# A SwiGLU FFN in 2x2 block algebra: two weight sums moved into accumulating DMAs, and 18 of 22 gate/up tiles in the algebra in place of 14

## The chip, the core and the metric

The kernel runs on one core of one Trainium2 chip. The metric is the device time of one execution in microseconds, taken as the median over several runs. Profiles are of one execution each, so a profile has a time of its own.

## The reference

One layer of a hybrid decoder, in float32: a token mixer (a gated recurrence and a gated delta rule side by side), then a feed-forward network. The change touches only the feed-forward network:

```
v = rms_norm(h, pre_ffn_w)                          # (512 tokens, 1024)
gate, up = split(v @ w_gate_up, 2)                  # w_gate_up: (1024, 2 * 2816)
f = (silu(gate) * up) @ w_down                      # w_down: (2816, 1024)
out = h + rms_norm(f, post_ffn_w)
```

Matrix products are made in about float32 accuracy: each operand x is split into a high part (x rounded to fp32r, the tiles `whi`, `vhi`) and a low part (x minus the high part, `wlo`, `vlo`), and a product is three fp32r matmuls, high x high, high x low and low x high.

## The kernel before

The program is written for one core with a scheduler that sets the order on each engine and inserts the waits; a tile pool hands out buffers in turn, and a new tile waits until the last reader of the tile that had the buffer before it is done. Pools that matter here: `raw` (fresh weights, float32) has 2 buffers, `whi` and `wlo` (the split weights) have 3 each. ScalarE (ACT) makes every high part, VectorE (DVE) every low part. SyncE's queue (SP) issues the loads, in its order: a load whose buffer is not free holds back the loads behind it. GpSimd (POOL) has a queue of its own for DMAs.

The stages are: mixers, merge, output projection (`out_proj`), FFN gate/up (`ffn`), FFN down (`down`). In `ffn` the 2816 columns of gate and of up are 22 tiles `ft` of 128. A tile's weights are `w_gu[ft, 0]` (gate) and `w_gu[ft, 1]` (up), each 128 x 1024 (512 KB): the first 512 columns are the four blocks of 128 inputs of the upper half of the 1024 inputs, the other 512 those of the lower half. There are two kinds of tile.

- A **direct** tile loads gate and up with `wload` (one DMA of 512 KB each into a `raw` buffer, a split of 128x1024 on ACT and on DVE), and TensorE makes 2 x 8 x 3 = 48 matmuls of 512 columns (L116 to L118).
- A **Winograd** tile takes gate and up times the two halves of the inputs and the two halves of the tokens as a 2x2 block product with 7 products in place of 8 (`winograd`, L959). Each product is 4 x 3 = 12 matmuls of 256 columns (L1010 to L1012). Its seven weight operands, numbered 0 to 6, are blocks or sums of blocks; each is split by `operand` (L913) into half a `whi` and half a `wlo` buffer (128x512), so three buffers hold six operands, and a pair of operands waits for the products of the third pair before it. TensorE takes a tile's products in the order 0, 1, then 6 of the tile before, then 2, 3, 4, 5; `s15`, `s16`, `c22`, `c12`, `c21` are its evictions on DVE (128x256), and `flush` ends the tile before (silu and product).

Before, the four weight sums are made by DVE in `winograd`: two at once into `t13` (128x1024), then two into `t24` (128x512 each). Both are tiles of the pool `raw`:

```
self.tt(t13, raw[:, 1:3], raw[:, 0:2], ALU.subtract)
self.tt(t24[:, 0], B22, t13[:, 0], ALU.subtract)
self.tt(t24[:, 1], B21, t24[:, 0], ALU.subtract)
```

The name `raw` in `winograd` is something else: a slot of 128x4x512, one of two that take turns, `s` in the profile; four loads of 256 KB fill it. Tiles 0, 1, 4, 7, 10, 13, 16 and 19 are direct (`ft < 2 or ft % 3 == 1`), so the other 14 come in twos, a direct tile between.

Of the kernel before, what the change touches and what calls it, by code (L numbers as in the profile page):

```python
# [9 lines left out]
F32 = mybir.dt.float32  # L10
# [4 lines left out]
ALU = mybir.AluOpType  # L15

P = 128
# [6 lines left out]
NF = DFF // P  # L24
EPS = 1e-6
NEG = -30000.0
HG_LEVELS = (64, 32, 16, 8, 4, 2, 1)
HG_MASKS = (16, 8, 4, 2, 1)

# [14 lines left out]
class K:  # L44
# [570 lines left out]
    def hg_attn(self, c, out):  # L615
# [20 lines left out]
        yield  # L636
        for lev in HG_LEVELS[:-1]:
            v = lambda x: x.rearrange("p h (n two t) -> p (h n) two t", two=2, t=lev)
# [194 lines left out]
    def out_proj(self):  # L833
# [4 lines left out]
        for nh in range(2):  # L838
            for lst, tile_, nm in ((pmw, self.hct, "post_mix_w"), (pfw, self.st, "pre_ffn_w")):
                t = tile_()  # L840
                lst.append(t.rearrange("p h t -> p (h t)"))
                nc.gpsimd.dma_start(out=lst[nh], in_=self.I[nm][nh * 512:nh * 512 + 512].partition_broadcast(P))
        W = []
        for i in range(8):
# [9 lines left out]
            for j in range(2):  # L854
                raw = self.dct((P, 512))
                nc.sync.dma_start(out=raw, in_=self.I["w_out"][i, :, j * 512:j * 512 + 512])
                self.split(h_[:, j, :], l_[:, j, :], raw, nc.gpsimd if i % 2 else None)
            W.append((h_, l_))
        self.h = []
# [64 lines left out]
    def block_sums(self, A, tmp, dst):  # L924


        hi, lo = A
        H, L = slice(256, 512), slice(0, 256)
        g = self.nc.gpsimd
        out = dict(A11=(0, L), A12=(1, L), A22=(1, H))  # L930
        out = {n: [[x[i][:, k, t] for k in range(4)] for x in A] for n, (i, t) in out.items()}
        S_ = [([], []) for _ in range(4)]
        for j in (slice(0, 2), slice(2, 4)):
            def block(i, t, eng=None):
                a = tmp()
                self.tt(a, hi[i][:, j, t].bitcast(F32), lo[i][:, j, t].bitcast(F32), ALU.add, eng)
                return a

            def put(i, src):
                d = dst(i, j)  # L940
                self.split(d[0], d[1], src)
                for o, x in zip(S_[i], d):
                    o += [x[:, 0], x[:, 1]]

            a21, a22 = block(0, H), block(1, H)
            self.tt(a22, a21, a22, ALU.add)
            put(0, a22)
            a11 = block(0, L, g)
            self.tt(a21, a11, a21, ALU.subtract)
            put(2, a21)  # L950
            self.tt(a22, a22, a11, ALU.subtract)
            put(1, a22)
            a12 = block(1, L, g)
            self.tt(a12, a12, a22, ALU.subtract)
            put(3, a12)
        out.update({f"S{i + 1}": S_[i] for i in range(4)})
        return out

    def winograd(self, raw, A, c12, c21, c22):  # L959

        nc = self.nc
        with self.tc.high_priority(offset=200):
            B11, _, B22, B21 = (raw[:, i] for i in range(4))
            t13, t24 = (self.wp.tile([P, 1040], F32, tag="raw", name=self.name("raw"), bufs=2)[:, :1024]
                        .rearrange("p (i n) -> p i n", i=2) for _ in range(2))
            self.tt(t13, raw[:, 1:3], raw[:, 0:2], ALU.subtract)
            self.tt(t24[:, 0], B22, t13[:, 0], ALU.subtract)
            self.tt(t24[:, 1], B21, t24[:, 0], ALU.subtract)  # L970
            W = [[t.rearrange("p (k f) -> p k f", k=4) for t in self.operand(x)]
                 for x in (B11, t13[:, 0], t24[:, 0], B21, t13[:, 1], B22, t24[:, 1])]
        X, Wb, Y = (f((P, 256)) for f in (self.mm_ps, self.dps, self.hps))
        prod = lambda i, a, ps, start: self.product(i, W[i], A[a], ps, start)
        s1, s15, s16 = (self.ftmp() for _ in range(3))
        now = self.tc.high_priority

        def first():
            prod(0, "A11", X, True)
            with now():  # L980
                nc.scalar.copy(s1, X)
            prod(1, "S1", Wb, True)
            with now():
                self.tt(s15, Wb, s1, ALU.add)

        def second():
            prod(2, "S2", Y, True)
            with now():
                self.tt(s16, Y, s1, ALU.add)
            prod(3, "A12", X, False)  # L990
            prod(4, "S3", Y, False)
            with now():
                self.tt(c22, Y, s15, ALU.add)
            prod(5, "S4", Wb, False)
            with now():
                self.tt(c12, Wb, s16, ALU.add)

        def third():
            prod(6, "A22", Y, False)
            with now():  # L1000
                self.tt(c21, Y, s1, ALU.add)

        return X, first, second, third

    def product(self, i, W, A, ps, start):
        wh, wl = W
        ah, al = A
# [14 lines left out]
    def ffn(self):  # L1022

        nc = self.nc
        A = nc.scalar
        self.half = self.fhalf = None
        gt = []

        def gslot(i):
            if i % 4 == 0:  # L1030
                gt.append(self.slot((4, 13, 11, 12, 14, 15)[i // 4], [P, 4, S]))
            return gt[i // 4][:, i % 4, :]

        def mms(ps, w, ts):
            for k in range(KD):
                self.mm3(ps[:, ts], w[0][:, k, :], w[1][:, k, :], self.vhi[k // 4][:, k % 4, ts],
                         self.vlo[k // 4][:, k % 4, ts], k == 0, k == KD - 1)

        load = lambda ft, gu: self.wload(self.I["w_gu"][ft, gu], (P, KD, P))

        def evac(t, g, u):
            with self.tc.high_priority():
                self.sigmoid(t, g)
                self.tt(t, t, g, ALU.mult)
                self.tt(t, t, u, ALU.mult)

        bank = lambda gu: self.hps((P, 512)) if gu else self.mm_ps()

        first = [(0, 0), (0, 1), (1, 0)]
        ws = {p: load(*p) for p in first}  # L1050
        pss = {p: bank(p[1]) for p in first}
        for half in range(2):
            for p in first:
                mms(pss[p], ws[p], slice(half * 256, half * 256 + 256))
        sp = [self.slot(i, [P, 4, 2, 256]) for i in (14, 15)]
        sp = iter([t[:, i] for t in sp for i in range(4)])
        so = [self.slot(i, [P, 2, 4, 256], F32R) for i in range(4)]
        L = self.block_sums((self.vhi, self.vlo), lambda: next(sp), lambda i, j: (so[i][:, 0, j], so[i][:, 1, j]))
        lo, hi = slice(0, 256), slice(256, 512)
        pending = None  # L1060

        def flush():
            nonlocal pending
            if pending:
                X, third, g, u, t = pending
                third()
                A.activation(t[:, lo], X, AF.Exp, scale=-1.0)
                A.activation(t[:, hi], g[:, hi], AF.Exp, scale=-1.0)
                A.activation(t, t, AF.Ln, bias=self.one)
                A.activation(t, t, AF.Exp, scale=-1.0)  # L1070
                self.tt(t[:, lo], t[:, lo], X, ALU.mult)
                self.tt(t[:, hi], t[:, hi], g[:, hi], ALU.mult)
                self.tt(t, t, u, ALU.mult)
            pending = None

        for ft in range(NF):
            if ft < 2 or ft % 3 == 1:
                for gu in range(2):
                    if (ft, gu) not in ws:
                        pss[ft, gu] = bank(gu)  # L1080
                        mms(pss[ft, gu], load(ft, gu), slice(0, S))
                    if gu == 0:
                        flush()
                evac(gslot(ft), pss[ft, 0], pss[ft, 1])
                continue
            with self.tc.high_priority():
                raw = self.slot(5 + ft % 2, [P, 4, 512])

                for gu in range(2):
                    src = self.I["w_gu"][ft, gu].rearrange("p (a b) -> p a b", a=2)  # L1090
                    nc.sync.dma_start(out=raw[:, gu], in_=src[:, 0])
                    nc.sync.dma_start(out=raw[:, 3 - gu], in_=src[:, 1])
            g, u = self.hct((P, 512)), self.hct((P, 512))
            X, p1, p2, p3 = self.winograd(raw, L, u[:, lo], g[:, hi], u[:, hi])
            p1()
            flush()
            p2()
            pending = X, p3, g, u, gslot(ft)
        flush()
        self.gt = gt  # L1100
# [116 lines left out]
def layouts(i):  # L1217
# [28 lines left out]
    t = np.arange(P)  # L1246
    cm = [np.eye(P), t[:, None] <= t[None, :], np.where(t[:, None] <= t[None, :], 0.0, NEG)]
    blk = lambda h: ((t[:, None] // (2 * h) == t[None, :] // (2 * h))
# [22 lines left out]
```

## Time and profile before

| | |
|---|---|
| median of 3 runs | 860.11 us (859.06 to 862.14) |
| the profiled execution | 856.85 us, its span 855.1 us |
| FFN gate/up, first direct matmul to first matmul of the down stage | 482.36 to 715.53 us of the span |
| of it the steady stretch, tiles 4 to 20 | 526.37 to 712.00 us, six periods of one direct and two Winograd tiles |
| FFN down | 715.53 to about 847 us |

The span runs from the first to the last instruction; 1.75 us lie outside it. A period of the steady stretch begins with the first 512-column matmul of a direct tile.

### The profile page before, as it was taken

Reading aid. Unit: us, or ns where it says so; the run is one execution under the profiler, and the core shown is the slowest. Engines: PE = TensorE matmul, PEld = TensorE weight load, DVE = VectorE, ACT = ScalarE, POOL = GpSimd, SP = SyncE. Lnnn points to the kernel's source line nnn. Section 1 sums busy time; section 2 is a strip of 40 time slices with the busy share of each in tenths; the row PEclk is TensorE's granted clock in tenths of the full one; section 3 lists DMA queues with packets and bytes.
Section 4 is the critical chain, followed back from the end, with each engine's and each line's share of the span. In section 5 each row is a group of like instructions: output and inputs, shape, how many; then the busy total and the mean of one; then the engine's idle time right before and its main releaser. Section 6 shows DMA issues by size and latency. Waiting matters only on the chain.

```text
span 855.1 us, 12329 instructions
## 1 busy us (share of the span) xinstructions
PE 823.5 (96%) x4684; PEld 695.8 (81%) x4684; DVE 581.2 (68%) x903; ACT 487.2 (57%) x888; POOL 137.4 (16%) x182
## 2 busy tenths in 40 slices
PE   8998999999999998999999999999999999999995
PEld 8986887788877777888888898999999998876774
DVE  4598779518478788622574697787787787557545
ACT  6648788755475666755443464545555456445443
POOL 1320168300054545300010300000000000000000
PEclk9999999959999999999999999999999999999999
DMA  8425432501051123522211313232322405556552
GB/s 295 152 75 196 125 101 95 155 26 50 26 185 50 50 75 99 170 91 88 96 62 50 124 41 109 91 107 99 122 76 100 148 5 168 174 173 212 182 170 101
DMA packets 34315, 96.43 MB, mean 113 GB/s; under 512 B 4112, under 2 KB 4528, under 8 KB 34128
## 3 DMA queue, kind: packets, MB, share of 16 engines
q1 hardware_dynamic: 32112, 88.65, 31.5%
q0 software_dynamic: 2144, 6.99, 3.1%
q8 instruction: 37, 0.61, 0.3%
q14 instruction: 22, 0.18, 0.1%
HBM read 90.90 MB, written 4.73 MB: 112 GB/s over the span
## 4 chain that ended last, share of the span: by engine, by line
PE 56%; DMA 11%; DVE 9%; POOL 4%; ACT 4%; issue 3%; DVEq 0%; ACTq 0%; SPq 0%; POOLq 0%
DMA raw<-in_w_down_dram 8%; PE mm L117 7%; PE mm L118 7%; PE mm L116 7%; POOL s L147 4%; DVE wlo L109 4%; ACT whi L108 3%; DVE hct L147 2%; PE hps L1011 2%; PE hps L1010 2%; PE hps L1012 2%; PE mm L869 2%; PE mm L868 2%; PE mm L867 2%; PE hps L118 2%
## 5 line engine op out<-in xcount | busy, mean ns | idle before, releaser
L109 DVE TENSOR_TENSOR wlo<-raw,whi 128x1024 fp32r<-128x1024 f32 x108 | 135.7, 1257 | 121.3 <-ACT whi L108 120.2
L116 PE MATMUL mm<-s,whi 128*128 128x512 f32 (+1 forms) x496 | 195.3, 394 | 0.0
L117 PE MATMUL mm<-s,whi 128*128 128x512 f32 (+1 forms) x496 | 195.0, 393 | 0.0
L118 PE MATMUL mm<-s,wlo 128*128 128x512 f32 (+1 forms) x496 | 194.6, 392 | 0.1
L108 ACT CAST whi<-raw 128x1024 fp32r<-128x1024 f32 x108 | 113.0, 1046 | 92.3 <-PE mm L117 39.1
L118 PEld LDWEIGHTS mm<-s,wlo 128*128 128x128 f32 x496 | 94.0, 190 | 19.8 <-DVE wlo L109 0.6
L116 PEld LDWEIGHTS mm<-s,whi 128*128 128x128 f32 x496 | 94.2, 190 | 19.3 <-issue 0.2
L117 PEld LDWEIGHTS mm<-s,whi 128*128 128x128 f32 x496 | 94.1, 190 | 18.7
L147 POOL TENSOR_TENSOR s<-s,dct 128x512 f32<-128x512 f32 (+1 forms) x9 | 12.7, 1435 | 391.6 <-DVE s L150 360.6
L121 ACT CAST whi<-raw 128x512 fp32r<-128x512 f32 (+1 forms) x64 | 38.9, 617 | 30.2 <-PE mm L1011 10.1
L121 ACT CAST whi<-s 128x512 fp32r<-128x512 f32 x42 | 25.9, 617 | 47.1 <-PE mm L117 21.4
L1010 PE MATMUL hps<-s,whi 128*128 128x256 f32 x168 | 47.2, 281 | 0.4 <-DVE hct L147 0.4
L1011 PE MATMUL hps<-s,whi 128*128 128x256 f32 x168 | 47.2, 281 | 0.1
L1012 PE MATMUL hps<-s,wlo 128*128 128x256 f32 x168 | 46.9, 279 | 0.0
L147 POOL TENSOR_TENSOR hct<-s 128x256 f32<-128x256 f32 (+1 forms) x55 | 43.4, 818 | 21.3 <-DVE hct L147 8.3
L147 DVE TENSOR_TENSOR wlo<-raw,whi 128x512 fp32r<-128x512 f32 (+1 forms) x64 | 43.5, 688 | 3.9 <-ACT whi L121 3.0
L147 DVE TENSOR_TENSOR hct<-hct,s 128x256 f32<-128x256 f32 (+1 forms) x63 | 32.7, 559 | 2.0 <-ACT hct L609 1.0
L147 POOL TENSOR_TENSOR s<-s 128x126 f32<-128x126 f32 (+22 forms) x62 | 32.3, 521 | 9.7 <-DMA s<-scr 4.9
L1010 PEld LDWEIGHTS hps<-s,whi 128*128 128x128 f32 x168 | 31.5, 188 | 0.9 <-DVE hct L147 0.6
L1011 PEld LDWEIGHTS hps<-s,whi 128*128 128x128 f32 x168 | 31.6, 188 | 0.6 <-DVE s L147 0.3
L1012 PEld LDWEIGHTS hps<-s,wlo 128*128 128x128 f32 x168 | 31.7, 189 | 0.0
L1011 PE MATMUL mm<-s,whi 128*128 128x256 f32 x112 | 31.5, 281 | 0.0
(329 smaller groups left out, 1943.2 us busy)
## 6 DMA issues: line engine op xcount, KB each, us to landing
raw<-in_w_in_a_dram SPq DMA_DIRECT2D x44, 512.0 KB, 3.4
raw<-in_w_down_dram SPq DMA_DIRECT2D x44, 512.0 KB, 3.4
s<-in_w_gu_dram SPq DMA_DIRECT2D x56, 256.0 KB, 4.0
raw<-in_w_gu_dram SPq DMA_DIRECT2D x16, 512.0 KB, 3.5
raw<-in_w_o_dram SPq DMA_DIRECT2D x8, 512.0 KB, 3.4
dct<-in_w_out_dram SPq DMA_DIRECT2D x16, 256.0 KB, 3.4
raw<-in_w_iab_dram SPq DMA_DIRECT2D x8, 260.0 KB, 5.9
s<-in_xT_dram SPq DMA_DIRECT2D x8, 256.0 KB, 6.0
```

What stands on the lines that cost most here:

```text
L108: nc.scalar.copy(hi[:, :n], raw[:, :n])
L109: nc.vector.tensor_tensor(out=lo[:, :n], in0=raw[:, :n], in1=hi[:, :n].bitcast(F32), op=ALU.subtract)
L116: mm(ps, lh, rh, start=start, stop=False)
L117: mm(ps, lh, rl, start=False, stop=False)
L118: return mm(ps, ll, rh, start=False, stop=stop)
L121: self.nc.scalar.copy(hi, src)
L147: (eng or self.nc.vector).tensor_tensor(out=out, in0=a, in1=b, op=op)
L867: T.matmul(ps, mh, wh, start=k == 0, stop=False)
L868: T.matmul(ps, mh, wl, start=False, stop=False)
L1010: mm(ps, wh[:, k, :], ah[k], start=start and k == 0, stop=False, skip_group_check=True)
L1011: mm(ps, wh[:, k, :], al[k], start=False, stop=False, skip_group_check=True)
L1012: mm(ps, wl[:, k, :], ah[k], start=False, stop=k == 3, skip_group_check=True)
```

## The change

1. **Two sums by DMA.** Per Winograd tile, a tile `u13` of the pool `raw` (128x2x512) is loaded by SP with the first halves of gate and up (512 KB). Then GpSimd issues a DMA that adds the whole of up (512 KB from DRAM) to it: `u13[0]` becomes gate's first half plus up's first, `u13[1]` up's first plus up's second. The slot's loads are one of 512 KB (gate) and one of 256 KB (up's second half).
2. **The other two sums** stay on DVE, in place in the slot (128x512 each): `U2 = B22 + u13[0]`, and `B21 = B21 + U2` once operand 3, which is the old B21, is split.
3. **Signs** in `block_sums` and in three evictions follow, so that the sums are plus.
4. **Direct tiles** are 0, 1, 8 and 15. The 18 Winograd tiles come in runs of six: 2 to 7, 9 to 14, 16 to 21.

```diff
+DIRECT = (0, 1, 8, 15)
...
-    def winograd(self, raw, A, c12, c21, c22):
+    def winograd(self, raw, u13, A, c12, c21, c22):
...
-            B11, _, B22, B21 = (raw[:, i] for i in range(4))
-            t13, t24 = (self.wp.tile([P, 1040], F32, tag="raw", name=self.name("raw"), bufs=2)[:, :1024]
-                        .rearrange("p (i n) -> p i n", i=2) for _ in range(2))
-            self.tt(t13, raw[:, 1:3], raw[:, 0:2], ALU.subtract)
-            self.tt(t24[:, 0], B22, t13[:, 0], ALU.subtract)
-            self.tt(t24[:, 1], B21, t24[:, 0], ALU.subtract)
-            W = [[t.rearrange("p (k f) -> p k f", k=4) for t in self.operand(x)]
-                 for x in (B11, t13[:, 0], t24[:, 0], B21, t13[:, 1], B22, t24[:, 1])]
+            B11, B21, B22, U2 = (raw[:, i] for i in range(4))
+            self.tt(U2, B22, u13[:, 0], ALU.add)
+            W = [self.operand(x) for x in (B11, u13[:, 0], U2, B21, u13[:, 1], B22)]
+            self.tt(B21, B21, U2, ALU.add)
+            W = [[t.rearrange("p (k f) -> p k f", k=4) for t in w] for w in W + [self.operand(B21)]]
...
-            if ft < 2 or ft % 3 == 1:
+            if ft in DIRECT:
...
                 raw = self.slot(5 + ft % 2, [P, 4, 512])
-
-                for gu in range(2):
-                    src = self.I["w_gu"][ft, gu].rearrange("p (a b) -> p a b", a=2)
-                    nc.sync.dma_start(out=raw[:, gu], in_=src[:, 0])
-                    nc.sync.dma_start(out=raw[:, 3 - gu], in_=src[:, 1])
+                u13 = self.wp.tile([P, 1040], F32, tag="raw", name=self.name("raw"), bufs=2)[:, :1024]
+                u13 = u13.rearrange("p (i n) -> p i n", i=2)
+                g, u = (self.I["w_gu"][ft, gu].rearrange("p (a b) -> p a b", a=2) for gu in range(2))
+                nc.sync.dma_start(out=u13, in_=self.I["w_gu"][ft, :, :, :512].rearrange("g p n -> p g n"))
+                nc.sync.dma_start(out=raw[:, :2], in_=g)
+                nc.sync.dma_start(out=raw[:, 2], in_=u[:, 1])
+
+                nc.gpsimd.dma_start(out=u13, in_=u, accum_op=ALU.add)
```

Every line number behind the first hunk is one higher than before. The next lists show an engine's instructions in program order: line, operation, tile written, tiles read, shape. Here `raw_n` is a tile of the pool `raw` and `s_n` the slot of a Winograd tile.

DVE before the change, tiles 8 (`raw_5112`, `raw_5113`) and 9 (`raw_5229`, `raw_5230`, `s_792_5222`): the three sums of tile 9 stand among the low parts (`wlo`) of tile 8 and its evictions (`hct` from `dps` or `hps`).

```order
L147 TENSOR_TENSOR wlo_5130<-raw_5112,whi_5129 128x512
L147 TENSOR_TENSOR wlo_5130<-s_773_5105,whi_5129 128x512
L147 TENSOR_TENSOR raw_5229<-s_792_5222 128x1024
L147 TENSOR_TENSOR hct_5142<-dps_5140,hct_5142 128x256
L147 TENSOR_TENSOR wlo_5136<-raw_5113,whi_5135 128x512
L147 TENSOR_TENSOR wlo_5136<-s_792_5222,whi_5135 128x512
L147 TENSOR_TENSOR hct_5143<-hps_5141,hct_5142 128x256
L147 TENSOR_TENSOR raw_5230<-s_792_5222,raw_5229 128x512
L147 TENSOR_TENSOR raw_5230<-s_792_5222,raw_5230 128x512
```

DVE after the change, in the run 9 to 14, tiles 11 (`raw_5542`) and 12 (`raw_5676`, `s_841_5675`): U2 of tile 12 is the third row, s15 of tile 11 the fifth, operand 4 of tile 11 (`u13[1]`) the sixth.

```order
L148 TENSOR_TENSOR hct_5417<-dps_5441,hct_5443 128x256
L148 TENSOR_TENSOR s_824_5541<-s_824_5541 128x512
L148 TENSOR_TENSOR s_841_5675<-s_841_5675,raw_5676 128x512
L148 TENSOR_TENSOR s_792_5290<-s_792_5290,hct_5303 128x512
L148 TENSOR_TENSOR hct_5576<-dps_5574,hct_5576 128x256
L148 TENSOR_TENSOR wlo_5563<-raw_5542,whi_5562 128x512
L148 TENSOR_TENSOR wlo_5563<-s_824_5541,whi_5562 128x512
```

The three sums of a tile (one of 1024, two of 512) have become two of 512, the first of which (U2) reads the accumulated `u13`; it stands ahead of operand 4 of the tile before it, which is the last reader of that tile's `u13`.

DVE after the change at the start of the first run, tiles 3 (`raw_4547`, `s_707_4546`) and 4 (`raw_4678`, `s_721_4677`):

```order
L148 TENSOR_TENSOR hct_4439<-hct_4467,hps_4466 128x256
L148 TENSOR_TENSOR hct_4439<-dps_4465,hct_4468 128x256
L148 TENSOR_TENSOR s_721_4677<-s_721_4677,raw_4678 128x512
L148 TENSOR_TENSOR wlo_4564<-s_707_4546,whi_4563 128x512
L148 TENSOR_TENSOR wlo_4564<-raw_4547,whi_4563 128x512
L148 TENSOR_TENSOR s_707_4546<-s_707_4546 128x512
```

U2 of tile 4 stands ahead of operands 3 and 4 of tile 3 (the low parts `wlo_4564`). Before the change tile 4 was direct and had no sum there.

SP's queue after the change, tiles 11 and 12; L1089 is the load of `u13`, L1090 and L1091 fill the slot:

```order
L1089 DMA raw_5542<-in_w_gu_dram 128x2x512
L1090 DMA s_824_5541<-in_w_gu_dram 128x1024
L1091 DMA s_824_5541<-in_w_gu_dram 128x512
L1089 DMA raw_5676<-in_w_gu_dram 128x2x512
L1090 DMA s_841_5675<-in_w_gu_dram 128x1024
L1091 DMA s_841_5675<-in_w_gu_dram 128x512
```

A tile has three loads here where it had four of 256 KB, and the load of `u13` has come in ahead of the slot's; the accumulating DMA (L1093) is alone on GpSimd's queue, whose other work between the first Winograd tile's and the last's is four adds of `block_sums` and one load of `post_ffn_w`, all ahead of the second accumulation.

## Rows read from the trace of the kernel before

**Rows 1.** The page: the span, and each engine's busy time.

```profile
span 855.1 us, 12329 instructions
PE 823.5 (96%) x4684; PEld 695.8 (81%) x4684; DVE 581.2 (68%) x903; ACT 487.2 (57%) x888; POOL 137.4 (16%) x182
```

**Rows 2.** Busy time per stretch: one period, the whole steady stretch, the down stage.

```profile
core 0: us, PE busy (x) PEld busy (x) DVE busy (x) ACT busy (x) POOL busy (x), PEclk, DMA share, GB/s
557.59:588.50 30.91, 30.91 (x218) 28.83 (x217) 24.26 (x41) 15.99 (x29) 0.00 (x0) 1.00 0.29 100
...
526.37:712.00 185.63, 185.51 (x1299) 172.73 (x1297) 145.93 (x242) 96.20 (x175) 0.00 (x0) 1.00 0.29 97
716.00:842.00 126.00, 121.56 (x513) 94.03 (x512) 72.49 (x100) 62.12 (x98) 0.00 (x0) 1.00 0.55 178
```

**Rows 3.** TensorE in order of time: start, length, line, tile; first matmuls of blocks.

```profile
588.50 0.40 PE L116 MATMUL mm<-s,whi 128*128 128x512 f32 x1
...
594.05 0.28 PE L1010 MATMUL hps<-s,whi 128*128 128x256 f32 x1
...
595.49 0.39 PE L116 MATMUL hps<-s,whi 128*128 128x512 f32 x1
...
601.03 0.28 PE L1010 MATMUL mm<-s,whi 128*128 128x256 f32 x1
...
609.47 0.28 PE L1010 MATMUL mm<-s,whi 128*128 128x256 f32 x1
```

**Rows 4.** DVE in order of time, back to back, in Winograd tiles.

```profile
602.43 0.68 DVE L147 TENSOR_TENSOR wlo<-s,whi 128x512 fp32r<-128x512 f32 x1
603.03 1.22 DVE L147 TENSOR_TENSOR raw<-s 128x1024 f32<-128x1024 f32 x1
604.17 0.42 DVE L147 TENSOR_TENSOR hct<-dps,hct 128x256 f32<-128x256 f32 x1
...
618.09 0.42 DVE L147 TENSOR_TENSOR s<-s,hct 128x256 f32<-128x256 f32 x1
618.43 0.42 DVE L147 TENSOR_TENSOR hct<-hps,hct 128x256 f32<-128x256 f32 x1
```

**Rows 5.** DMA issues: queue, count, KB each, median us from issue to landing.

```profile
s<-in_w_gu_dram SPq DMA_DIRECT2D x40, 256.0 KB, 4.0
raw<-in_w_gu_dram SPq DMA_DIRECT2D x10, 512.0 KB, 3.6
...
s<-gd POOLq DMA_DIRECT2D x1, 1024.0 KB, 6.5
scr<-dct POOLq DMA_DIRECT2D x1, 1024.0 KB, 9.3
scr<-s POOLq DMA_DIRECT2D x2, 512.0 KB, 3.8
st<-in_pre_ffn_w_dram POOLq DMA_DIRECT2D x2, 256.0 KB, 3.6
```

**Rows 6.** Start of the Winograd tiles: DVE and TensorE in order of time.

```profile
497.99 1.21 DVE L109 TENSOR_TENSOR wlo<-raw,whi 128x1024 fp32r<-128x1024 f32 x1
506.88 0.28 PE L1010 MATMUL mm<-s,whi 128*128 128x256 f32 x1
```

**Rows 7.** Start of the down stage: last Winograd matmul, ScalarE, first down matmul.

```profile
713.30 0.28 PE L1012 MATMUL hps<-s,wlo 128*128 128x256 f32 x1
...
714.13 1.04 ACT L108 CAST whi<-raw 128x1024 fp32r<-128x1024 f32 x1 [1.30 <-DVE wlo L109]
715.08 1.01 ACT L121 CAST hct<-s 128x256 fp32r<-128x256 f32 x3
...
715.53 0.50 PE L1121 MATMUL dps<-whi,hct 128*128 128x512 f32 x1 [1.95 <-ACT hct L121]
```

**Rows 8.** All that GpSimd does from 470 to 720 us.

```profile
478.73 6.02 POOL L147 TENSOR_TENSOR s<-s,s 128x512 f32<-128x512 f32 x4 [46.29 <-PE mm L868]
488.36 0.55 POOL L1131 DMA_DIRECT2D st<-in_post_ffn_w_dram  x1 [3.62 <-DVE hct L150]
```

More of the change, by code (lines that the diff above doesn't have):

```diff
@@ L945, in block_sums @@
             a21, a22 = block(0, H), block(1, H)
-            self.tt(a22, a21, a22, ALU.add)
+            self.tt(a22, a21, a22, ALU.subtract)
             put(0, a22)
@@ L953, in block_sums @@
             a12 = block(1, L, g)
-            self.tt(a12, a12, a22, ALU.subtract)
+            self.tt(a12, a12, a22, ALU.add)
             put(3, a12)
@@ L983, in first @@
             with now():
-                self.tt(s15, Wb, s1, ALU.add)
+                self.tt(s15, Wb, s1, ALU.subtract)
         def second():
@@ L992, in second @@
             with now():
-                self.tt(c22, Y, s15, ALU.add)
+                self.tt(c22, s15, Y, ALU.subtract)
             prod(5, "S4", Wb, False)
             with now():
-                self.tt(c12, Wb, s16, ALU.add)
+                self.tt(c12, Wb, s16, ALU.subtract)
         def third():
@@ L1087, in ffn @@
                 raw = self.slot(5 + ft % 2, [P, 4, 512])
-                for gu in range(2):
-                    src = self.I["w_gu"][ft, gu].rearrange("p (a b) -> p a b", a=2)
-                    nc.sync.dma_start(out=raw[:, gu], in_=src[:, 0])
-                    nc.sync.dma_start(out=raw[:, 3 - gu], in_=src[:, 1])
+                u13 = self.wp.tile([P, 1040], F32, tag="raw", name=self.name("raw"), bufs=2)[:, :1024]
[5 more added lines that the diff above has]
+                nc.gpsimd.dma_start(out=u13, in_=u, accum_op=ALU.add)
             g, u = self.hct((P, 512)), self.hct((P, 512))
-            X, p1, p2, p3 = self.winograd(raw, L, u[:, lo], g[:, hi], u[:, hi])
+            X, p1, p2, p3 = self.winograd(raw, u13, L, u[:, lo], g[:, hi], u[:, hi])
             p1()
```

## The prediction

> **What bounds the kernel now.** I read the page first: TensorE is busy 96% of the span [rows 1]. Ends of matmuls are modelled there, so this alone proves little. Second, busy time by stage: in the steady stretch of the FFN TensorE is busy 185.51 of 185.63 us at clock 1.00, DVE 145.93 (79%), ACT 96.20 (52%), the DMA engines 29%, GpSimd nothing [rows 2]. Third, to be sure that TensorE sets the pace, I read its starts: gate of a direct tile starts at 588.50 and the next block at 594.05, up at 595.49 and the next at 601.03 [rows 3]. That is 5.55 and 5.54 us for 24 matmuls each, 0.231 us apart. From 601.03 to 609.47 lie six products, 1.41 us each, and the seventh takes 594.05 to 595.49. The period made of these (11.09 + 2 x 9.88 = 30.85) is the period measured, 30.91 [rows 2]. So nothing waits there, and what counts is how many matmuls TensorE is given, as long as its operands come in time.
>
> **The change part by part.** Spans of one profiled execution make the sum; that execution took 856.85 us, 3.26 below the median of 860.11, and the result is carried over to the median.
>
> *Products.* A direct tile costs 11.09 us, a Winograd tile 8.44 + 1.44 = 9.88 [rows 3]. Four tiles change kind: 4 x 1.21 = **4.8 us less**, if TensorE stays fed.
>
> *DVE.* Back to back, a 128x512 operation follows the one before by 0.60 us, one of 128x1024 by 1.14, one of 128x256 by 0.34 [rows 4]. A Winograd tile before is 1.14 + 2 x 0.60 for sums, 7 x 0.60 for low parts, 5 x 0.34 for evictions, and 2 x 0.34 + 0.60 to end the tile before: 9.5 us. After, the 1.14 is gone: 8.4 us per 9.88 of TensorE, 85%. In runs of six there is no direct tile to catch up in, but work alone leaves 1.5 us a tile. Before, 9.5 of 9.88 would have left little; so the runs rest on the DMA sums. I cost this at nothing, hidden behind the products. ACT has the same seven casts a tile and 48% to spare. The changed signs cost nothing: the same operations.
>
> *DMA traffic.* A tile moved 1 MB and now moves 1.75 MB, 0.5 of it added to what is there. At 29% load [rows 2] this fits by volume; the down stage runs at 55% and lands its loads. The SP queue gives up a load a tile; GpSimd's has no work behind the accumulations until the end but one load [rows 8], so its wait for `u13` holds up nobody.
>
> *The new wait.* Call L the time from a free `u13` buffer to U2's input: the load (512 KB, 3.6 us by the `raw` row [rows 5]; the nearest with rows of 2 KB is the slot's, 4.0 in bursts of four), two hand-overs of about 0.1 us (my estimate), and X, the accumulation. The trace has none. Below, X is a plain GpSimd DMA of 512 KB, 3.8 us; above, the slowest of 1024 KB, 9.3 [rows 5]. An accumulation reads the tile as well as DRAM. From 256 KB (3.6) to 1024 KB (6.5) 768 KB more cost 2.9 us, so 512 KB more read cost 1.9: I take X = 3.8 + 1.9 = **5.7**, L = 3.6 + 0.2 + 5.7 = **9.5**, with 7.6 and 13.1 for the ends.
>
> The Trainium skill, "Collectives: The Full Stack", section "The bandwidth ceiling: the fold count and why AG ≠ RS ≠ AR", says that an add in the DMA path costs no time for the adding, but needs two source reads that share one ring, and so runs at half a copy's rate. With its 31 GB/s an engine, X would by my estimate be 3.8 + 1.1 = 4.9 and the sum below 0.6 us better, at most; no row here shows an accumulation.
>
> U2 is what waits, and DVE works in order: everything behind U2 waits too. At the start of a run and at every other tile inside it, U2 of the next tile stands ahead of operand 4 of this one, which frees the buffer that the tile after next needs. So waits form a chain: U2, operand 4, L, U2. First run: the direct weight's low part frees tile 3's buffer at 499.2 [rows 6]. Then U2(3) at 499.2 + L, operand 4 of tile 2 2.5 later (three operations and its own 0.69), U2(4) after another L, operand 4 of tile 3 1.9 later, U2(5) after L, operand 4 of tile 4 2.2 later, U2(6) after L: 505.8 + 4L. Behind U2(6) stand two evictions and operand 5 of tile 5, 2.0 us, for the 27th product of the run: 506.88 [rows 6] + 26 x 1.41 + 1.9 of delay (next paragraph) = 545.4. So L may be 9.4. In the later runs tiles 9 and 10 have a direct tile's time for their sums; the chain starts with operand 4 of tile 9, 1.4 us after the direct tile's last matmul, and has three links: 1.4 + 2 x 2.2 + 3L against 26 x 1.41 - 2.0 = 34.7, L at most 9.6. Beyond **about 9.5** each microsecond of L costs 4 + 3 + 3 = 10 us; below it nothing. My L lies on the edge.
>
> *Start of the first run.* Before, the 13 products from 506.88 to 526.37, where the steady stretch begins [rows 2, 6], took 19.49 us, 1.2 more than 13 x 1.41. After, U2(3) holds DVE until 499.2 + 9.5 = 508.7; U2, four more operations and then the half of a block sum that product 2 needs half-way through take 5 x 0.60 + 0.69 = 3.7, to 512.4, where 510.4 would be in time (506.88 + 2.5 x 1.41): 1.9 late. That is **0.7 more**.
>
> *Start of the down stage.* The last product's last matmul starts at 713.30, the first of the down stage at 715.53: ACT makes the third down weight's high part at 714.13, held by DVE's low part of the second, and only then the left operand [rows 7]. The third's buffer is free when the last product ends (713.30 + 0.28, so 713.6). `u13` is done with two operands before `t24` was, so the first down weights load earlier, DVE is through with the second sooner, and I take **0.5 less**; nothing, if ACT's order finds another wait.
>
> Sum: -4.8 + 0.7 - 0.5 = **-4.6 us**: 852.25 in the profile, 855.5 as a median.
>
> **The rivals.** 0.3% (2.6 us) is about what a measurement of this kernel can tell from no change.
>
> *The accumulation is late (slower).* If X is 7.0, as a little above the 6.5 row, L is 10.8, the chains cost 13, and the sum is +8.4: 868.5. It decides from X = 6.2, where 10 x 0.46 eats the 4.6; at 9.3 (L 13.1) it would be 36 - 4.6, 891. For it: both 1024 KB rows exceed 6.2, 6.5 and 9.3 [rows 5], slot loads run in the same microseconds, and one late U2 delays the next buffer. Against it: the 3.8 row, and 71% idle DMA engines.
>
> *The chains eat the gain (same).* X between 5.9 and 6.4: 858 to 863.
>
> *DVE becomes the bound (same).* At 8.4 of 9.88 us every wait on an eviction in the middle of a tile costs slack. If a Winograd tile took 10.2 us, 18 x 0.32 = 5.8 would cancel the products: 861.3. Against it: before, two tiles of 9.5 followed each other with no gap on TensorE.
>
> *The accumulation is quick (faster still).* X = 3.8: U2(3) at 506.8, the start is in time, and its 1.2 us of delay are gained: -4.8 - 1.2 - 0.5 = -6.5, 853.6.
>
> **How the numbers follow.** Forecast 0.38, quick accumulation 0.10, the two that end in no change 0.20 together, late accumulation 0.32. Faster is 0.48, same 0.20, slower 0.32. The likeliest case's own range is 853.5 to 857.5. For 8 in 10 the low end is 853 (a quick accumulation; 0.05 below it) and the high end 870, the chains at L = 10.95; 0.12 lies beyond, towards 891.
>
> **What would show it.** Right: in the steady part of a run seven products every 9.88 us with no idle time of TensorE; U2 (`s<-s,raw`) in DVE's list with idle time released by the accumulating DMA, some microseconds per tile at a run's start, and operands still in time; accumulations landing in 5 to 6 us. Wrong: TensorE idle before a Winograd matmul, released by a low part, at the fourth or fifth tile of each run; that would be the late accumulation, its landing above 6.2. DVE busy without gaps while TensorE waits would be the DVE rival. If U2 never waits, the quick one holds. The sum would be wrong in its first term if a product in a run took other than 1.41 us.

## The result

The changed kernel takes **885.58 us** (median of 4 runs, 884.14 to 892.9), beside 859.59 us of the kernel before on the same chip: 1.0318 times as long, 95% interval 1.0254 to 1.0381. The prediction, 855.5 with a range up to 870, was wrong; of its rivals the late accumulation comes nearest in mechanism and time.

The profiled execution took 884.97 us, its span is 883.2. From its page: span and busy time [rows 1]; three groups of instructions (busy, mean ns | idle time ahead of them, and what ended it); DMA issues [rows 5].

```profile
span 883.2 us, 12751 instructions
...
PE 831.1 (94%) x4828; PEld 707.4 (80%) x4828; DVE 578.4 (65%) x941; ACT 497.6 (56%) x916; POOL 153.0 (17%) x200
...
L1008 PE MATMUL hps<-s,whi 128*128 128x256 f32 x216 | 63.7, 295 | 21.0 <-DVE hct L148 20.7
...
L1093 POOL DMA_DIRECT2D raw<-in_w_gu_dram x18 | 15.6, 864 | 224.8 <-DVE wlo L148 116.5
L148 DVE TENSOR_TENSOR s<-s,raw 128x512 f32<-128x512 f32 x18 | 12.5, 693 | 55.1 <-DMA raw<-in_w_gu_dram 45.9
...
raw<-in_w_gu_dram SPq DMA_DIRECT2D x26, 512.0 KB, 3.5
raw<-in_w_gu_dram POOLq DMA_DIRECT2D x18, 512.0 KB, 6.6
s<-in_w_gu_dram SPq DMA_DIRECT2D x18, 512.0 KB, 4.4
```

U2 (`s<-s,raw`) makes DVE wait 45.9 us for accumulations (its other 8.2 us of idle time, in three tiles, end with the slot's load), and TensorE waits 20.7 us for `hct`, an **eviction**, not for a low part as the prediction had it. An accumulation lands 6.6 us after its issue, a `u13` load after 3.5. The stretches of the gate/up stage, and one behind a wait, by window (columns as in [rows 2]):

```profile
504.00:575.00 71.00, 63.99 (x494) 62.98 (x493) 50.50 (x97) 36.49 (x69) 3.44 (x4) 0.93 0.54 146
575.00:657.00 82.00, 72.98 (x553) 69.96 (x552) 55.25 (x107) 40.76 (x77) 5.16 (x6) 0.98 0.57 146
657.00:742.00 85.00, 76.88 (x568) 73.45 (x566) 58.35 (x111) 42.24 (x80) 5.16 (x6) 0.96 0.52 136
...
596.21:599.00 2.79, 2.79 (x13) 2.79 (x14) 1.15 (x2) 0.00 (x0) 0.86 (x1) 0.50 0.85 258
```

TensorE is idle in all three, DVE too, and the granted clock, 1.00 before, falls: right after a wait of 2.79 us it is 0.50, the 1.2 GHz level. One link of the chain, tiles 11 to 13, in the timeline (start, length, engine):

```profile
606.11 0.38 SPq L1089 DMA_DIRECT2D raw<-in_w_gu_dram  x1
...
610.13 0.86 POOL L1093 DMA_DIRECT2D raw<-in_w_gu_dram  x1 [11.51 <-DVE wlo L148]
...
616.74 0.69 DVE L148 TENSOR_TENSOR s<-s,raw 128x512 f32<-128x512 f32 x1 [3.24 <-DMA raw<-in_w_gu_dram]
617.35 0.68 DVE L148 TENSOR_TENSOR s<-s,hct 128x512 f32<-128x512 f32 x1
617.96 0.42 DVE L148 TENSOR_TENSOR hct<-dps,hct 128x256 f32<-128x256 f32 x1
618.29 0.68 DVE L148 TENSOR_TENSOR wlo<-raw,whi 128x512 fp32r<-128x512 f32 x1
618.89 0.68 DVE L148 TENSOR_TENSOR wlo<-s,whi 128x512 fp32r<-128x512 f32 x1
619.49 0.41 DVE L148 TENSOR_TENSOR hct<-hps,hct 128x256 f32<-128x256 f32 x1
619.83 1.28 DVE L148 TENSOR_TENSOR wlo<-s,whi 128x512 fp32r<-128x512 f32 x2
621.03 0.42 DVE L148 TENSOR_TENSOR hct<-hps,hct 128x256 f32<-128x256 f32 x1
...
619.00 0.38 SPq L1089 DMA_DIRECT2D raw<-in_w_gu_dram  x1
...
621.59 0.36 PE L1008 MATMUL hps<-s,whi 128*128 128x256 f32 x1 [2.51 <-DVE hct L148]
```

The load of tile 12's `u13` is issued at 606.11, the accumulation at 610.13, and U2 of tile 12 runs at 616.74: L, the time from the load's issue to U2, is 10.6 us. Behind it DVE makes operand 4 of tile 11 (618.29), and 2.3 us after U2 the load for tile 13 goes out: a link of 12.9 us, where TensorE needs 9.88 a tile. The last DVE row is s16 of tile 11, 4.3 us behind U2. A tile's fifth product, the one of operand 4, adds to the bank of PSUM (where TensorE puts its sums) that s16 reads, so TensorE, through with the fourth, is idle for 2.51 us and begins it at 621.59. Twelve tiles have such a wait. In two of them, 9 and 16, it comes right behind a direct tile; in three, 6, 13 and 20, U2 of the next tile waited last for the slot's load, which landed some tenths of a microsecond behind an accumulation of 7.5 to 8.5 us.

**Where the time went.** From the first Winograd matmul to the first of the down stage it was 208.65 us (506.88 to 715.53 [rows 6, 7]). Now, by TensorE's timeline, it is 237.75:

```profile
504.25 0.28 PE L1008 MATMUL mm<-s,whi 128*128 128x256 f32 x1
...
742.00 0.50 PE L1122 MATMUL dps<-whi,hct 128*128 128x512 f32 x1 [1.65 <-ACT hct L122]
```

Consecutive matmul starts further apart than the usual 0.117 us (0.231 for 512 columns) are counted as a wait where more than 0.25 us is added, else as a short delay:

| term | us |
|---|---|
| four tiles of the other kind | -4.8 |
| TensorE's waits, 25.2 where 1.1 were | +24.1 |
| short delays, 10.5 where 0.4 were | +10.1 |
| last Winograd matmul to first down matmul | -0.3 |
| sum, as measured | +29.1 |

The short delays are the clock in the main: 8.8 of the 10.5 us lie in six stretches, 20.5 us together, in which the granted clock was 0.50.

Outside, the first Winograd matmul came 2.6 us earlier (over all runs below it lies between 504.2 and 509.9, with the same program ahead), and what follows took 1.6 longer: 28.1 in the spans.

### The profile page after: what moved, and what is told of

Its sections match the earlier page's. It is cut to its first block, busy times and chain, and to the rows that moved or that the text cites. A ratio compares the mean times of both kernels' runs of the same rounds, so it can differ in the third digit from the quotient of the medians.

```text
span 883.2 us, 12751 instructions
## 1 busy us (share of the span) xinstructions
PE 831.1 (94%) x4828; PEld 707.4 (80%) x4828; DVE 578.4 (65%) x941; ACT 497.6 (56%) x916; POOL 153.0 (17%) x200
## 4 chain that ended last, share of the span: by engine, by line
PE 39%; DMA 21%; DVE 16%; ACT 5%; POOL 4%; issue 4%; DVEq 0%; ACTq 0%; POOLq 0%; SPq 0%
DMA raw<-in_w_gu_dram 9%; DMA raw<-in_w_down_dram 8%; PE mm L117 6%; PE mm L118 6%; PE mm L119 6%; POOL s L148 4%; DVE s L148 4%; DVE wlo L110 4%; DVE wlo L148 3%; DVE hct L148 3%; ACT whi L109 3%; DMA s<-in_w_gu_dram 2%; PE mm L869 2%; PE mm L870 2%; PE mm L868 2%
## 5 line engine op out<-in xcount | busy, mean ns | idle before, releaser
L117 PE MATMUL mm<-s,whi 128*128 128x512 f32 (+1 forms) x464 | 182.6, 393 | 0.0
L118 PE MATMUL mm<-s,whi 128*128 128x512 f32 (+1 forms) x464 | 182.1, 393 | 0.0
L119 PE MATMUL mm<-s,wlo 128*128 128x512 f32 (+1 forms) x464 | 181.7, 392 | 0.0
L122 ACT CAST whi<-s 128x512 fp32r<-128x512 f32 x90 | 53.5, 617 | 67.2 <-PE hps L1009 25.5
L1008 PE MATMUL hps<-s,whi 128*128 128x256 f32 x216 | 63.7, 295 | 21.0 <-DVE hct L148 20.7
L1009 PE MATMUL hps<-s,whi 128*128 128x256 f32 x216 | 62.5, 289 | 1.4 <-DVE s L148 1.4
L1010 PE MATMUL hps<-s,wlo 128*128 128x256 f32 x216 | 62.3, 288 | 0.0
L1008 PEld LDWEIGHTS hps<-s,whi 128*128 128x128 f32 x216 | 42.2, 195 | 23.7 <-ACT s L1067 11.7
L148 DVE TENSOR_TENSOR wlo<-s,whi 128x512 fp32r<-128x512 f32 x90 | 59.7, 684 | 0.9
L1093 POOL DMA_DIRECT2D raw<-in_w_gu_dram x18 | 15.6, 864 | 224.8 <-DVE wlo L148 116.5
L148 DVE TENSOR_TENSOR s<-s,raw 128x512 f32<-128x512 f32 x18 | 12.5, 693 | 55.1 <-DMA raw<-in_w_gu_dram 45.9
L1009 PEld LDWEIGHTS hps<-s,whi 128*128 128x128 f32 x216 | 42.5, 197 | 1.7 <-DVE s L148 1.6
L1008 PE MATMUL dps<-s,whi 128*128 128x256 f32 x144 | 42.3, 294 | 0.0
L1009 PE MATMUL dps<-s,whi 128*128 128x256 f32 x144 | 42.0, 292 | 0.0
```

What stands on the lines that cost most here:

```text
L117: mm(ps, lh, rh, start=start, stop=False)
L118: mm(ps, lh, rl, start=False, stop=False)
L119: return mm(ps, ll, rh, start=False, stop=stop)
L122: self.nc.scalar.copy(hi, src)
L148: (eng or self.nc.vector).tensor_tensor(out=out, in0=a, in1=b, op=op)
L1008: mm(ps, wh[:, k, :], ah[k], start=start and k == 0, stop=False, skip_group_check=True)
```

## The experiments

Theory A: U2, waiting for a late accumulation, stands in DVE's order ahead of work that TensorE needs, and ahead of operand 4, so that the waits form a chain. Theory B: DVE's work is the bound. Theory D: the accumulation is late wherever its sum is made. "Waits" and "short delays" are counted as above, in us, from the first to the last Winograd matmul; ratios are to the kernel before on the same chip. The granted clock fell there in runs 2 (two stretches), 4 (one), 6 (five), 7 and 11 (one each); in the others it was 1.00, and their short delays are short waits.

| run | us | ratio (95%) | waits | short delays |
|---|---|---|---|---|
| 1 plain copy | 863.83 | 1.0070 (1.0043 to 1.0098) | 9.2 | 1.3 |
| 2 eight direct tiles | 870.77 | 1.0150 (1.0113 to 1.0186) | 11.8 | 3.8 |
| 3 sums on DVE, 18 tiles | 857.04 | 0.9986 (0.9966 to 1.0006) | 0.8 | 1.6 |
| 4 more buffers | 874.39 | 1.0195 (1.0160 to 1.0231) | 14.7 | 2.7 |
| 5 U2 on GpSimd | 866.16 | 1.0078 (1.0047 to 1.0110) | 8.5 | 1.2 |
| 6 both sums on GpSimd | 889.52 | 1.0333 (1.0290 to 1.0375) | 26.9 | 9.7 |
| 7 halves | 881.22 | 1.0250 (1.0201 to 1.0299) | 20.4 | 2.8 |
| 8 U2 in place | 855.32 | 0.9960 (0.9943 to 0.9978) | 1.4 | 0.2 |
| 9 in place, 20 tiles | 852.54 | 0.9919 (0.9896 to 0.9942) | 0.0 | 0.0 |
| 10 sums on DVE, 20 tiles | 857.55 | 0.9970 (0.9952 to 0.9989) | 0.8 | 2.5 |
| 11 U2 in a single buffer | 878.30 | 1.0224 (1.0190 to 1.0257) | 18.0 | 3.0 |
| 12 in place, eight direct | 864.31 | 1.0052 (1.0032 to 1.0071) | 4.3 | 0.8 |

**1. What the adding costs.**

```diff
-                nc.gpsimd.dma_start(out=u13, in_=u, accum_op=ALU.add)
+                nc.gpsimd.dma_start(out=u13, in_=u)
```

> The changed kernel with GpSimd's DMA as a plain copy of up over u13 instead of an accumulation; the two sums are left out, all waits and bytes from DRAM stay. Theory A (a late accumulation: U2 stands in DVE's queue ahead of the evictions that TensorE needs, and each link of the chain takes L + 2.2 us, 12.6 in the changed kernel): L falls from about 10.4 to 3.5 + 0.3 + 3.8 = 7.6, a link to 9.8, about a tile's 9.88; TensorE's waits in the gate/up stage fall from 25 us to under 6, its half-clock time from 10.5 to under 3, and the time to 853 to 862. Theory B (DVE's work is the bound of runs of six): nothing of DVE's work changes, so the time stays above 875. Theory C (SP's loads and their bytes are late, not the adding): above 875 as well.

This kernel leaves out the two sums, so its output is not the layer's. DMA issues of this run:

```profile
raw<-in_w_gu_dram SPq DMA_DIRECT2D x26, 512.0 KB, 3.5
raw<-in_w_gu_dram POOLq DMA_DIRECT2D x18, 512.0 KB, 4.6
```

The same transfer without the add lands in 4.6 us, not in the 3.8 of [rows 5]; the add costs 2.0 more. L was mostly 8.5 to 9.4 (523.07 to U2 at 531.78, 597.30 to 606.68), and the waits fell from 25.2 to 9.2. The time is a little above what theory A expected, far below B and C: with the same loads, bytes and order the lateness of the accumulation is worth most of the loss, and L near 9 is still too long.

**2. The accumulations without the long runs.**

```diff
-            if ft in DIRECT:
+            if ft < 2 or ft % 3 == 1:
```

> The changed kernel with the eight direct tiles of before (0, 1, 4, 7, 10, 13, 16, 19): the accumulations without the longer runs. Theory A1 (only the chain inside a long run costs): pairs have a direct tile's 11.1 us to catch up, so the time is that of before, 857 to 864. Theory A2 (also the first tile after a direct one costs, because its U2 holds DVE for 7 to 9 us during the direct tile and the work behind it piles up; the trace after shows 2.0 to 2.9 us of TensorE's waiting and 1.3 of half clock at two such places): six such places, 3.5 to 4.2 us each, 878 to 885. Theory B (DVE's work): as A1 or a little faster, DVE has 14 x 1.1 us less than before.

Between the two: seven waits of 0.9 to 2.5 us, one for a block sum and six in the first tile after a direct one. So short runs lose too, against the prediction, by which tiles after a direct one have "a direct tile's time for their sums", but less than six full places.

**3. The long runs without the accumulations.** In the kernel before:

```diff
-            if ft < 2 or ft % 3 == 1:
+            if ft in (0, 1, 8, 15):
```

> The kernel before with direct tiles 0, 1, 8 and 15 alone: 18 tiles in the block algebra, all four sums on DVE, no accumulation. Theory A (waits on DMA were the loss): no such wait, four tiles x 1.21 us less, so 853 to 858, if 9.5 us of DVE per 9.88 leave enough; with small waits up to 862. Theory B (DVE is the bound in runs of six): a Winograd tile takes over 10.2 us, 862 to 880, and DVE has no idle time in the runs.

No accumulation, no slowdown; within what can be told, the time is that of before (its gate/up stage, counted as above, took 205.39 us where 208.65 were). Theory B falls here, and the prediction's "the runs rest on the DMA sums" with it.

**4. Buffers that run ahead.**

```diff
+                if ft < 16 and ft % 2 or ft in (17, 19):
+                    u13 = self.slot(14 + ft // 2 % 2 if ft < 16 else 15, [P, 2, 512])
+                else:
```

> The changed kernel, with u13 of every second tile (up to tile 19) in a slot that is free at the time, in place of the pool of two buffers that the direct tiles use too. Nothing else changes. Theory A (the chain needs operand 4 of one tile to free the buffer for the tile after next): loads and accumulations run a tile or more ahead, U2 waits less than 1 us a tile, TensorE's waits in the gate/up stage fall below 5 us, time 851 to 857. If the slot loads, not u13, come last: 857 to 868. Theory B (DVE's work): above 875.

The expectation failed, in good part through my choice of buffers: the accumulation of tile 3, into a slot that `block_sums` also uses, was issued at 522.54 only, and TensorE waited 8.9 us for operand 1. Of the 5.8 us that are left, 2.7 lie in one wait after a direct tile (599.20). The run says little on the chain inside a run of tiles.

**5, 6. The sums on GpSimd.**

```diff
-            self.tt(U2, B22, u13[:, 0], ALU.add)
+            self.tt(U2, B22, u13[:, 0], ALU.add, nc.gpsimd)
```

> The changed kernel with U2 = B22 + u13[0] made by GpSimd in place of DVE; loads, accumulations, buffers and tiles are the same. Theory A (the place of the wait: in DVE's order U2 stands some nine instructions, 4.7 us, ahead of s16, which TensorE's fifth product of the same tile needs): now the first DVE instruction that waits for the accumulation is operand 1 of the next tile, which stands behind s16, and operand 4, which frees the u13 buffer, no longer stands behind a wait of the next tile; L of 10 to 12 us fits into the two tiles, 19.8 us, for which a buffer serves. TensorE's waits in the gate/up stage fall from 25 to under 4 us, accumulations still land in 6 to 7 us; time 851 to 858. Theory D (the accumulation is late wherever its sum is made, two buffers are too few): 868 to 885. Theory B (DVE's work): 870 or more, since only 0.6 us a tile leave DVE.

Run 6 does the same to `self.tt(B21, B21, U2, ALU.add)` as well.

> As the run before, with the second sum, B21 + U2, on GpSimd too: DVE's work in a tile falls from 8.4 to 7.2 us. Theory A: no further gain, as DVE's work is not the bound, 851 to 858; a loss of some microseconds if the second sum, which waits for operand 3, stands in GpSimd's queue ahead of the next accumulation. Theory B (DVE's work): 5 us or more faster than the run before.

One instruction moved takes two thirds of the waits away (25.2 to 8.5), against B and D; the time, 866.16, is above A's range all the same. What stayed lies again ahead of the fifth product. Timeline of run 5, GpSimd and DVE:

```profile
523.60 1.77 POOL L148 TENSOR_TENSOR s<-s,raw 128x512 f32<-128x512 f32 x1 [7.80 <-DMA raw<-in_w_gu_dram]
...
523.52 2.40 DVE L148 TENSOR_TENSOR wlo<-s,whi 128x512 fp32r<-128x512 f32 x2
525.84 0.41 DVE L148 TENSOR_TENSOR hct<-hps,hct 128x256 f32<-128x256 f32 x1
```

Beside GpSimd's add two low parts take 2.40 us where 1.28 is usual, and s16 (525.84) comes that much later. Run 8, which has no adds on GpSimd, has one wait in place of these ten. With both sums on GpSimd nothing is left of the gain: DVE's work fell by 1.2 us a tile and the time rose by 23, so work on DVE was not the bound; which of GpSimd's waits costs most there was not taken apart.

**7. The accumulation in halves.**

```diff
-                nc.gpsimd.dma_start(out=u13, in_=u, accum_op=ALU.add)
+                for i in range(2):
+                    nc.gpsimd.dma_start(out=u13[:, i], in_=u[:, i], accum_op=ALU.add)
```

The load of `u13` is halved in the same way.

> The changed kernel with the load of u13 in two of 256 KB and the accumulation in two of 256 KB, first half first; U2 needs only the first. Theory A: U2's input comes 2 us or more earlier, a link is 10 to 10.7 us in place of 12.6, TensorE's waits halve: 862 to 873. Theory D (what counts is when the whole buffer is through, or GpSimd's time per issue, 0.86 us, twice): 880 to 890.

From its DMA issues:

```profile
raw<-in_w_gu_dram POOLq DMA_DIRECT2D x36, 256.0 KB, 6.1
```

256 KB land 6.1 us after their issue, hardly sooner than 512 KB (the first half, which is all that U2 needs, after 5.8): L fell to about 9.1, not by 2 us or more, the waits to 20.4, not to half, and the time, 1.025 times that of before in place of 1.032, lies in D's range.

**8. U2 in place.**

```diff
-            B11, B21, B22, U2 = (raw[:, i] for i in range(4))
-            self.tt(U2, B22, u13[:, 0], ALU.add)
-            W = [self.operand(x) for x in (B11, u13[:, 0], U2, B21, u13[:, 1], B22)]
+            B11, B21, B22, _ = (raw[:, i] for i in range(4))
+            U2 = u13[:, 0]
+            W = [self.operand(x) for x in (B11, U2)]
+            self.tt(U2, B22, U2, ALU.add)
+            W += [self.operand(x) for x in (U2, B21, u13[:, 1], B22)]
```

> The changed kernel with U2 made by DVE in place, over u13[0], once operand 1 (which is u13[0]) is split. So U2 can't stand in DVE's order ahead of operands 0 and 1 of its tile, which wait for weight buffers; the first instruction that waits for an accumulation is operand 1, behind s16 of the tile before; operand 4 stands ahead of the next tile's. DVE's work is the same as in the changed kernel, GpSimd adds nothing. Theory A (the place of U2 in DVE's order): TensorE's waits in the gate/up stage fall from 25 to under 4 us although the accumulations land in 5.5 to 7 us as before; 852 to 858. Theory E (the 10 us of waits that were left with U2 on GpSimd do not come from GpSimd's adds, which ran beside low parts of 1.0 to 1.2 us in place of 0.6): 864 to 868. Theory D (the accumulation is late wherever the sum stands): 870 or more.

The page's busy time and issues; then a window in the first run of tiles (columns as in [rows 2]); then three of GpSimd's accumulations and, in DVE's order of the same place, s16, operands 0 and 1 and U2:

```profile
PE 820.0 (96%) x4828; PEld 698.6 (82%) x4828; DVE 578.6 (68%) x941; ACT 496.2 (58%) x916; POOL 152.1 (18%) x200
...
raw<-in_w_gu_dram POOLq DMA_DIRECT2D x18, 512.0 KB, 6.4
```

```profile
507.00:580.00 73.00, 73.00 (x576) 70.92 (x575) 57.66 (x109) 42.25 (x83) 5.16 (x6) 1.00 0.65 170
```

```profile
595.22 0.86 POOL L1095 DMA_DIRECT2D raw<-in_w_gu_dram  x1 [8.42 <-DVE wlo L148]
605.52 0.86 POOL L1095 DMA_DIRECT2D raw<-in_w_gu_dram  x1 [9.44 <-DVE s L148]
615.15 0.86 POOL L1095 DMA_DIRECT2D raw<-in_w_gu_dram  x1 [8.78 <-DVE wlo L148]
...
593.61 0.42 DVE L148 TENSOR_TENSOR hct<-hps,hct 128x256 f32<-128x256 f32 x1
593.95 0.68 DVE L148 TENSOR_TENSOR wlo<-s,whi 128x512 fp32r<-128x512 f32 x1
594.55 0.68 DVE L148 TENSOR_TENSOR wlo<-raw,whi 128x512 fp32r<-128x512 f32 x1
595.26 0.69 DVE L148 TENSOR_TENSOR raw<-s,raw 128x512 f32<-128x512 f32 x1
```

The accumulations land no sooner (6.4), the loads and bytes are the same, and so is DVE's work (578.6 us busy, 578.4 in the changed kernel), yet TensorE runs the first six tiles without a gap at clock 1.00, and accumulations come every 9.6 to 10.3 us, at TensorE's pace. U2 now stands behind s16, where it waits for nothing in the whole stage. One wait of 1.4 us is left, after a direct tile. This kernel is faster than before, by 0.2 to 0.6%, and the gate/up stage takes 203.62 us: the prediction's sum was 208.65 - 4.8 + 0.7 - 0.5 = 204.05.

**9, 10. Twenty tiles.** Tiles 0 and 1 alone direct: `DIRECT = (0, 1)` in run 8's kernel; `if ft < 2:` in the kernel before.

> The run before with direct tiles 0 and 1 alone: 20 tiles in the block algebra in one run. Theory A with DVE at 85%: two tiles x 1.21 us less and two starts after a direct tile fewer, so 2 to 5 us below the run before. Theory B (without direct tiles to catch up in, DVE's work becomes the bound): same as the run before or slower.

> The kernel before with direct tiles 0 and 1 alone, all sums on DVE, no accumulation: DVE has 9.5 us of work per tile of 9.88. If the work fits, 6 x 1.21 = 7.3 us less than before, 851 to 855; if it fits only with a direct tile now and then (18 tiles gave 0.9986 of before), no gain over the 18 tiles or slower, 857 to 865.

Run 9 is the fastest, 0.6 to 1.0% below before, with no wait between its Winograd matmuls. Run 10 gains less; so with 20 tiles the accumulations are worth about 0.5%, while with 18 the intervals of runs 3 and 8 overlap. One window of it:

```profile
530.00:700.00 170.00, 169.88 (x1428) 168.41 (x1427) 164.90 (x307) 104.80 (x204) 0.00 (x0) 1.00 0.32 102
```

DVE is busy 164.90 of 170.00 us, 97%, and TensorE is hardly held: 2.5 us of short delays in the whole run of tiles, at clock 1.00.

**11. U2 in a single buffer.**

```diff
+            U2 = self.tp.tile([P, 512], F32, tag="u2", name=self.name("u2"), bufs=1)
```

> The changed kernel with U2 in a buffer of its own, one for all tiles: U2 of the next tile has to wait until B21 + U2 of this one is made, so it moves back in DVE's order by some six instructions, still ahead of s16; in every other tile operand 4 now stands ahead of it. Theory A: the chain of load, accumulation, U2 and operand 4 is cut at every other tile, the waits ahead of s16 partly stay: 860 to 872, between the changed kernel and U2 in place. Theory D: 880 or more.

Slower than A expected, and short of D: U2 moved back by one operation at most, to 3.7 us (611.35 to 615.03) and 2.5 us (600.90 to 603.37) ahead of s16, where it had been 4.3 and 2.5, and 18.0 us of waits stayed. Cutting the chain at every other tile alone is not enough; the place ahead of s16 counts.

**12. In place, eight direct tiles.** `DIRECT = (0, 1, 4, 7, 10, 13, 16, 19)` in run 8's kernel.

> U2 in place, with the eight direct tiles of before: the kernel with eight direct tiles and accumulations that took 870.8 us, with U2 moved. Theory A (its 12 us over the kernel before came from U2's place in DVE's order, after each direct tile): 856 to 861, the time of before, TensorE's waits in the gate/up stage under 4 us; with 18 tiles 855.3 was measured, so 4 x 1.21 us more would be 860. Theory A3 (what costs after a direct tile is that the load of u13 waits for the direct weight's buffer, so the accumulation is late there wherever U2 stands): 865 to 871.

Between the two: run 2's loss of 12.3 us against the kernel before has become 4.3, and 4.3 us of waits stay, four of them, each after a direct tile. Moving U2 does not mend those. The first of them, in tile 5 behind direct tile 4 (DVE, the `u13` load, ACT's operand 1, s16, TensorE):

```profile
522.48 1.23 DVE L110 TENSOR_TENSOR wlo<-raw,whi 128x1024 fp32r<-128x1024 f32 x1 [0.21 <-ACT whi L109]
523.73 0.38 SPq L1091 DMA_DIRECT2D raw<-in_w_gu_dram  x1
...
534.82 0.62 ACT L122 CAST whi<-raw 128x512 fp32r<-128x512 f32 x1 [2.67 <-DMA raw<-in_w_gu_dram]
...
544.14 0.41 DVE L148 TENSOR_TENSOR hct<-hps,hct 128x256 f32<-128x256 f32 x1
...
544.61 0.39 PE L1010 MATMUL hps<-s,whi 128*128 128x256 f32 x1 [0.77 <-DVE hct L148]
```

The load goes out when the direct weight's low part has freed its buffer, the accumulation lands as late as 534.8, and from 535.5 on DVE works without a gap until s16. So A3's mechanism is there too, at about a third of run 2's loss.

## Why the prediction was wrong

**What bounds the kernel; products.** Right. A product took 1.41 us wherever TensorE was not held; four tiles of the other kind were worth 4.8.

**The deadline of U2: the step that failed.** "Behind U2(6) stand two evictions and operand 5 of tile 5, 2.0 us, for the 27th product." I read DVE's list as far as the next operand that a product needs. But a tile's fifth product adds to the bank that s16 reads, and s16 stands further behind U2. In the first run (U2 of tile 5, s16 of tile 4 and that product, the run's 19th; then U2 of tile 6, s16 of tile 5 and the 26th product):

```profile
531.92 0.69 DVE L148 TENSOR_TENSOR s<-s,raw 128x512 f32<-128x512 f32 x1 [3.01 <-DMA raw<-in_w_gu_dram]
536.20 0.42 DVE L148 TENSOR_TENSOR hct<-hps,hct 128x256 f32<-128x256 f32 x1
536.76 0.36 PE L1008 MATMUL hps<-s,whi 128*128 128x256 f32 x1 [2.31 <-DVE hct L148]
...
544.80 0.69 DVE L148 TENSOR_TENSOR s<-s,raw 128x512 f32<-128x512 f32 x1 [1.35 <-DMA raw<-in_w_gu_dram]
547.39 0.42 DVE L148 TENSOR_TENSOR hct<-hps,hct 128x256 f32<-128x256 f32 x1
548.27 0.28 PE L1008 MATMUL hps<-s,whi 128*128 128x256 f32 x1
```

From U2(5) to the 19th product it is 4.84 us, and 4.85 behind U2(12) in the timeline further up; U2(6) stands nearer to its s16, and the 26th product did not wait. So the chain is held a link earlier than where I looked. By the prediction's own chain U2(5) is at 503.6 + 3L, and L may be (506.88 + 18 x 1.41 + 1.9 - 4.85 - 503.6) / 3 = 8.57 in the first run, not 9.4; in the others U2(12) gives (18 x 1.41 - 4.85 - 3.6) / 2 = 8.46, not 9.6. So even the L I took, 9.5, would have cost 3 x 0.93 + 4 x 1.04 = 6.9 and made the forecast 862.4, no change, in place of 855.5. Runs 5 and 8, which change U2 alone (to GpSimd; in place, behind s16), show that its place decides.

**The direct tile's time: a second step that failed.** "In the later runs tiles 9 and 10 have a direct tile's time for their sums": they do not. Around direct tile 8 (the direct weight's low part, the load of tile 9's `u13`, U2 of tile 9, the load of tile 11's `u13`, s16 of tile 9, its fifth product):

```profile
572.06 1.23 DVE L110 TENSOR_TENSOR wlo<-raw,whi 128x1024 fp32r<-128x1024 f32 x1 [0.26 <-ACT whi L109]
573.31 0.38 SPq L1089 DMA_DIRECT2D raw<-in_w_gu_dram  x1
...
585.43 0.69 DVE L148 TENSOR_TENSOR s<-s,raw 128x512 f32<-128x512 f32 x1 [8.80 <-DMA raw<-in_w_gu_dram]
...
593.71 0.37 SPq L1089 DMA_DIRECT2D raw<-in_w_gu_dram  x1
...
595.74 0.41 DVE L148 TENSOR_TENSOR hct<-hps,hct 128x256 f32<-128x256 f32 x1
596.21 0.58 PE L1008 MATMUL hps<-s,whi 128*128 128x256 f32 x1 [2.79 <-DVE hct L148]
```

The load waits for the direct weight's buffer, U2(9) holds DVE until 585.43, and the work behind it makes s16 late. The chain of the later runs then starts 6.1 and 5.4 us behind the direct tile (593.71 against 587.61 in the run shown), not 1.4.

**The size of L.** Taken 9.5, measured 10.6: X is 6.6 in place of 5.7, and the load with its hand-over 4.0 in place of 3.8. The increment for the add was about right (2.0 in run 1, I took 1.9); the plain transfer under it was too small, 4.6 in place, not 3.8. The Trainium skill's rule ("Collectives: The Full Stack", section "The bandwidth ceiling: the fold count and why AG ≠ RS ≠ AR"), which the page gives for a ReduceScatter, two source reads at half rate, gave 1.1 for the add by my estimate; 2.0 was measured, and that decides.

The chain itself holds: a link is L + 2.3 us (I had 2.2). With L = 10.6, these limits and these starts it makes the 19th product of the three runs 3 x 2.03 = 6.1, 2 x 2.14 + 4.7 = 9.0 and 2 x 2.14 + 4.0 = 8.3 us late. Measured, waits and short delays together and without the start's 1.9, were 5.2, 8.6 and 8.2. The rest of the loss is not in this sum: the waits of tiles 6, 13 and 20, where the slot's load came last, and low clock behind the 19th product.

**What was left out: the clock.** Waits on TensorE were costed at their length. With them came 10.1 us more of short delays, mostly matmuls at the low level. The profile of before, at 1.00 throughout the steady stretch, has no price for it there, though the level stands in the same trace outside the stage (0.50 from 171 to 181 us). Of the waits of over 2 us some were followed by it (2.8 us at 596.21), others were not (2.5 us at 621.59). In runs 8 and 9, with one wait and with none, it is gone.

**The rivals.** The late accumulation was right in its chain, its U2 and the landing above 6.2 us. It was wrong in the releaser, low parts where it was evictions, and in the price: for X = 7.0 it gave 868.5. DVE as the bound is refuted by runs 3 and 10.

**Starts.** At the start of the first run TensorE waited 2.1 us for a block sum, which DVE makes behind U2 (0.4 at 508.25, 1.6 at 510.00); 1.9 was predicted. This first accumulation landed in 5.5 us, near the 5.7 assumed, which the later ones did not. The start of the down stage gave 0.3 of the 0.5.

## What to carry to other kernels

When an operation is made to wait for a longer chain, list all that stands behind it on its engine, and for each of those rows the first instruction elsewhere that needs it, evictions that free an accumulator as well as operands; the earliest of these deadlines counts. An operation that waits for a DMA belongs behind what it does not depend on, and a true dependency (here, in place over a tile that is read first) puts it there without a change of priorities. Waits on TensorE can cost more than their length where the granted clock falls behind them.

## What was not expected of the hardware

- An accumulating DMA of 512 KB landed after 6.6 us (5.5 to 6.8 in the other runs), the same DMA without the add after 4.6, and one of 256 KB with the add, issued in pairs, after 6.1.
- While GpSimd added two 128x512 tiles (1.3 to 1.8 us), a DVE operation of that shape begun beside it took up to 1.8 us in place of 0.7; DVE's evictions of 128x256 took 0.42 as ever.
- DVE busy 97% of the time kept TensorE fed, but for short delays (run 10).
